# High and low activations side by side: one 512-column product with the weights' high part, halves folded on the way out of PSUM, pools at 512-byte multiples

## The chip, the cores and the metric

One NeuronCore of a Trainium2 chip runs the whole program. TensorE (PE in the profile) multiplies a stationary 128x128 operand with a moving operand of up to 512 columns and writes PSUM; its weight loads have a row of their own (PEld). VectorE (DVE), ScalarE (ACT) and GpSimd (POOL) do the rest, and SyncE (SP) issues the transfers. The metric is device time in microseconds of one execution: 2353.95 us as the median of three runs of the kernel before (2352.78 to 2354.49).

## The reference, cut to what matters

A sequence of 256 tokens of width 1024 goes through ten stages. What the change touches are products `x @ w` with the 256-token activation `x`:

```python
def swiglu(h, w_gate, w_up, w_down):           # two layers, D_FF = 2816
    return (jax.nn.silu(h @ w_gate) * (h @ w_up)) @ w_down

def swiglu_2(x, w_in, w_out):                  # four times, 4096 wide
    gate, up = jnp.split(x @ w_in, 2, axis=-1)
    return (jax.nn.silu(gate) * up) @ w_out
```

Between them stand three mixers: `even` (gated spatial mixing and latent attention), `odd` (retention) and, twice, `hyb` (gated delta rule, block attention and windowed attention, merged by gates `x @ w_gate`). Each begins with products `x @ w_in` and ends with a product into the residual. All numbers are float32, and the kernel keeps nearly that accuracy: every product is made of three, `hi*hi + hi*lo + lo*hi`, where `hi` is the operand rounded to TensorE's fp32r format and `lo` the rest.

## The kernel before

Weights stream in units of at most 128x2048 numbers. `prep` (L135) loads a unit in two halves of 128x1024 (`raw`), ScalarE casts each to `hi` (L147), VectorE subtracts to get `lo` (L148). `pump` (L153) keeps four units ahead; `hi` and `lo` have four buffers each.

The activation, transposed, is `xT`: two tiles `xh` and `xl` of [128, 8, 256], made by `new_xT` (L427) and filled by `to_T` (L403). It takes part in products in two ways:

- `block` (L284): the activation is stationary and the weights are moving, 264 to 512 columns at a time. Result: tokens by features.
- `pair_tiles` (L339) called by `apair` (L330), and the same loop written out in `chunk` of `ffn` (L595-598): the weights are stationary, and 256 columns of `xh` or `xl` move past them. Result: features by tokens. Two feature tiles share one PSUM bank of 512 columns. Per feature tile there are 8 steps of `mm3` (L230), each three products of 256 columns: `hi` with `xh`, `hi` with `xl`, `lo` with `xh`.

A feed-forward stage (`ffn`) runs over chunks of 256 features: the first two by `head` with the first form, the others by `chunk` with the second: gate and up each into one `work` bank, SiLU by ScalarE and the product by VectorE straight out of PSUM, then a split into `hp` and, one chunk later, 24 products of 512 columns into the four accumulators `y` (`emit_down`). In `ffn` and `odd` the second form writes banks of the pool `work` (four of them), in `even` and `hyb` (where `gacc` is true) banks of the pool `acc` (four as well). Each call of `apair` hands its bank to a callback `cb`: in `hyb` a causal convolution (`cb_conv`, L1095), biases, or the tanh of a gate (`cb_g`, L1152).

Which instruction stands where on an engine is decided when the program is built, by a scheduler that merges the streams; each engine then works strictly through its own list.

SBUF pools are laid out one behind the other; the constants end with `colt` (L1523), whose width follows the number of column constants. In the built program `hi`, `lo`, `raw` and the `s` tiles used as operands start 480 bytes past a multiple of 512, `xh` and `xl` 288 bytes past one.

Of the kernel before, what the change touches and what calls it, by code (L numbers as in the profile page):

```python
# [4 lines left out]
F32 = mybir.dt.float32  # L5
F32R = mybir.dt.float32r
# [10 lines left out]
TAIL = 3  # L17
ACC = 4


# [95 lines left out]
class Net:  # L116
# [15 lines left out]

    # weight stream

# [66 lines left out]

    # tiles

    def tile(self, *free, dt=F32):
        n = int(np.prod(free))
        for tag, size, bufs in (("c", 16, 24), ("c2", 64, 10), ("s1", 272, 4), ("s2", 512, 22), ("s2x", 520, 2), ("s4", 1024, 11)):
            if n <= size:
                break
        else:
            raise ValueError(n)  # L210
        t = self.sp.tile([128, size], dt, tag=tag, bufs=bufs, name=tag)
        t = t[:, 0:n]
        if len(free) == 2:
            t = t.rearrange("p (a b) -> p a b", a=free[0])
        elif len(free) == 3:
            t = t.rearrange("p (a b c) -> p a b c", a=free[0], b=free[1])
        return t
# [6 lines left out]

    # short forms

# [47 lines left out]
    def bc(self, a, m):  # L274
        """[128, n] -> [128, n, m] with a stride of zero"""
        return a.unsqueeze(2).to_broadcast([128, a.shape[1], m]) if not self.recording else a

    def bh(self, a, h):
        """[128, n] -> [128, h, n] with a stride of zero"""
        return a.unsqueeze(1).to_broadcast([128, h, a.shape[1]]) if not self.recording else a  # L280

    # products with streamed weights

# [14 lines left out]
    def group(self, n, units, xT, cb):  # L298
        """out[token, n columns] of x @ w, one block of tokens after the other"""
        self.need_x(1)  # L300
        for b in range(2):
            yield from self.block(b, n, units, xT, cb)
        self.pump()

    def opening(self, groups):
        """the first groups of a stage: the second block of tokens comes late"""
        groups = [(n, self.col_units(key, cols), cb) for n, key, cols, cb in groups]
        self.need_x(0)
        for b in range(2):
            for n, units, cb in groups:  # L310
                for i, _ in enumerate(self.block(b, n, units, self.xT, cb)):
                    if b == 0 and i == 0 and units is groups[-1][1]:
                        self.need_x(1)
                    yield

    def col_units(self, key, cols, K=8, per=4):
        """cols: column ranges, or a function of the inputs that gives the [K * 128, n] slab"""
        units = []
        n = sum(c1 - c0 for c0, c1 in cols)
        for k in range(0, K, per):  # L320
            def fn(inp, k=k):
                return kslab2(key(inp), k, k + per, *cols)
            units.append(self.unit((per, n), fn) + (per,))
        return units
# [5 lines left out]
    def apair(self, key, cols, cb):  # L330
        """out[feature, token] of x @ w for two tiles of features"""
        def fn(inp):
            return kslab2(key(inp), 0, 8, *cols)
        u = self.unit((8, 256), fn)
        self.need_x(1)
        yield from self.pair_tiles(u, 0, self.xT, 8, cb)
        self.pump()

    def pair_tiles(self, u, c0, xT, K, cb):  # L339
# [10 lines left out]
    def outproj(self, key, r0, xT, y, first, last, K=4, per=2):  # L350
        """y[block][half] += x @ w for K tiles of the rows of w from r0"""
        units = []
        for k in range(0, K, per):
            def fn(inp, k=k):
                return kslab(key(inp), r0 + k, r0 + k + per, 0, 1024)
            units.append(self.unit((per, 1024), fn))
        for b in range(2):
            for k in range(K):
                hi, lo = units[k // per]
                for n in range(2):  # L360
                    self.mm3(y[b][n], tuple(t[:, k, 128 * b:128 * b + 128] for t in xT),
                             (hi[:, k % per, 512 * n:512 * n + 512], lo[:, k % per, 512 * n:512 * n + 512]),
                             first and k == 0, last and k == K - 1)
                if k % 2 == 1 and k < K - 1:
                    yield ("part", b)
            if b == 1:
                self.pump()
            yield ("block", b)

    def outlast(self, key, r0, xTs, y, first):  # L370
        """y += x @ w for the last rows of w, four tiles per item of xTs; in the last units the first block of tokens comes first"""
        n = 2 * len(xTs)
# [12 lines left out]
        for i in range(n - TAIL):  # L385
            w = unit(i)
# [16 lines left out]
    def to_T(self, src, b, dst, n, k0=0):  # L403
        """src [128 tokens, n * 128] into dst hi/lo [128, k, 256]"""
        for q in range(0, n, 4):
            m = min(4, n - q)
            ps = self.work()
            for k in range(m):
                self.tr(ps[:, 128 * k:128 * k + 128], src[:, 128 * (q + k):128 * (q + k) + 128])
            p = ps[:, 0:128 * m].rearrange("p (k t) -> p k t", k=m)  # L410
            s = slice(k0 + q, k0 + q + m), slice(128 * b, 128 * b + 128)
            self.split(dst[0][:, s[0], s[1]], dst[1][:, s[0], s[1]], p)
# [3 lines left out]

    # ends of stages

# [8 lines left out]
    def new_xT(self):  # L427
        self.xT = tuple(self.xp.tile([128, 8, 256], F32R, tag=t, bufs=1, name=t) for t in ("xh", "xl"))

# [74 lines left out]
    def finish_out(self, b, y):  # L504
        """the last layer norm: squares about the mean of the first half, the second half comes last"""
        c = self.how[3]
        z, h, junk = self.tile(1024), self.tile(1024), self.tile(1024)
# [37 lines left out]

    # the two-matrix gated feed-forward

    def ffn(self, nt, gate, up, down, nxt):
        """gate, up: (fn of inputs -> matrix, first column); down: fn -> matrix"""
        C = nt // 2  # L550
        self.gacc = False
        y = self.new_y()
# [34 lines left out]
        def chunk(c):  # L587
            ps = []
            for src in (gate, up):
                def fn(inp, src=src):  # L590
                    w, a, z = cols(src, c)(inp)
                    return kslab(w, 0, 8, a, z)
                hi, lo = self.unit((8, 256), fn)
                p = self.work()
                for j in range(2):  # L595
                    for k in range(8):
                        self.mm3(p[:, 256 * j:256 * j + 256], (hi[:, k, 128 * j:128 * j + 128], lo[:, k, 128 * j:128 * j + 128]),
                                 (self.xT[0][:, k], self.xT[1][:, k]), k == 0, k == 7)
                ps.append(p)
                while late:  # L600
                    late.pop(0)()
                if src is gate:
                    sg = self.tile(512)
                    self.act(sg, p, AF.Silu)
                    self.pump()
# [44 lines left out]

    # softmax over the last axis of [128, H, K]

    def softmax(self, s, H, K, scale, sink=None):
        """scale: a number, or one per row and head (positive)"""
        nm = self.tile(H)
# [21 lines left out]
    def p_T(self, p, H, nk):  # L677
        """p [128 q, H, nk * 128] -> [128 k, H, nk, 128 q]"""
        pT = self.tile(H, nk, 128)
# [11 lines left out]

    # layer 0 of the first block

    def even(self, nxt):
# [81 lines left out]
        def rope(x, b, H, dst):  # L776
            """x [128, H, 32]"""
            r = rt1 if b else rt
# [169 lines left out]

    # layer 1 of the first block

# [90 lines left out]

    # the mixer of the second block

    def hyb(self, l, nxt):
# [213 lines left out]
        def task_a():  # L1258
            while "kvc" not in events:
                yield "wait"  # L1260
            M = self.masks
            # beta and g
            beta, g = self.tile(2, 4), self.tile(2, 4)
# [27 lines left out]
            yield  # L1291
            # k in token layout, normalised; v in token layout; the lengths of q
            kt, vt, rq = [None] * 2, [None] * 2, [None] * 2
# [30 lines left out]
            yield  # L1324
            # decays: from j to i in [i, j], below the diagonal times beta and with the diagonal
            Dx, DT = [None] * 2, [None] * 2
# [37 lines left out]
            yield  # L1364
            # inverse of I + A: blocks of four in closed form, then doubled; X = inverse, Y = its transpose
            X, Y, Q = ([self.tile(512) for _ in range(2)] for _ in range(3))
# [142 lines left out]

    # the whole  # L1510

    def consts(self):
# [9 lines left out]
        if not self.recording:  # L1522
            self.colt = self.cp_.tile([128, max(self.collay.n, 1)], F32, name="colt")  # L1523

# [123 lines left out]
```

## Time and profile before

| what | value |
|---|---|
| median of three runs | 2353.95 us |
| profiled execution, first to last instruction (span) | 2348.7 us |
| PE busy | 2323.6 us (99%), 15966 products |
| weight loads (PEld) | 2140.5 us (91%) |
| DVE / ACT / POOL busy | 1393.4 / 1087.6 / 92.5 us |
| granted TensorE clock | 0.998 on average, the level of 2.4 GHz |
| weights read | 416.53 MB, 53.7% of the 16 DMA engines' time |

The profiled execution spans 2348.7 us; the page gives no time for what lies around the span, so its own total is known only through the runs, whose median is 5.25 us longer. Busy time of PE counts overlapping records once: one product's record is longer than the step from its start to the next one's, so steps have to be read from the starts.

### The profile page before, as it was taken

The numbers are of one execution on the slowest core, as the hardware profiler recorded it, in microseconds if no ns is written. First come the engines' busy times: TensorE is split into PE (matmuls) and PEld (weight loads), VectorE is DVE, ScalarE is ACT, GpSimd is POOL, SyncE is SP. The second block draws the span as 40 slices with busy tenths as digits, with TensorE's granted clock in tenths as the row PEclk, the third lists the DMA queues.
The fourth block names the chain that finished last, engine by engine and source line by source line (L and its number), as shares of the span: only waits on it lengthen the run. The fifth ranks groups of instructions, "written<-read, shape, count | busy, mean of one in ns | idle before, by whom it ended". The sixth has DMA issues, their size and how long they took to land.

```text
span 2348.7 us, 38487 instructions
## 1 busy us (share of the span) xinstructions
PE 2323.6 (99%) x15966; PEld 2140.5 (91%) x15966; DVE 1393.4 (59%) x1764; ACT 1087.6 (46%) x1530; POOL 92.5 (4%) x149
## 2 busy tenths in 40 slices
PE   8999999999999999999999999999999999999998
PEld 7789988889989999999998999899999999989997
DVE  6654475565455454786666454655457875664544
ACT  6644344354444444564445444444445544453433
POOL 4200000000000000000000000000000000000000
PEclk9999999999999999999999999999999999999999
DMA  7465555555556555553365555555555533665552
GB/s 244 139 206 189 189 193 173 191 170 190 192 171 217 195 184 176 185 174 118 105 201 199 194 183 193 182 201 189 188 181 185 186 105 107 189 206 188 189 189 90
DMA packets 120575, 419.51 MB, mean 179 GB/s; under 512 B 14408, under 2 KB 17224, under 8 KB 120400
## 3 DMA queue, kind: packets, MB, share of 16 engines
q1 hardware_dynamic: 120112, 416.53, 53.7%
q8 instruction: 125, 2.05, 0.3%
q10 hardware_dynamic: 288, 0.52, 0.1%
q14 instruction: 50, 0.41, 0.1%
HBM read 415.95 MB, written 1.05 MB: 178 GB/s over the span
## 4 chain that ended last, share of the span: by engine, by line
PE 97%; DVE 1%; POOL 1%; ACT 0%; DMA 0%; issue 0%; SPq 0%; POOLq 0%; DVEq 0%; ACTq 0%
PE work L228 52%; PE acc L228 42%; PE work L236 2%; DVE lo L148 0%; DMA raw<-in_w 0%; POOL c L271 0%; ACT hi L147 0%; DVE s L251 0%; POOL c L828 0%; POOL c L827 0%; POOL c L272 0%; DVE s L239 0%; PE work L1412 0%; ACT s L258 0%; DVE xl L239 0%
## 5 line engine op out<-in xcount | busy, mean ns | idle before, releaser
L148 DVE TENSOR_TENSOR lo<-raw,hi 128x1024 fp32r<-128x1024 f32 (+3 forms) x772 | 918.3, 1209 | 564.0 <-ACT hi L147 562.3
L147 ACT CAST hi<-raw 128x1024 fp32r<-128x1024 f32 (+3 forms) x772 | 783.4, 1037 | 922.2 <-issue 667.3
L228 PE MATMUL work<-xh,hi 128*128 128x256 f32 x2496 | 699.2, 280 | 0.0
L228 PE MATMUL work<-xl,hi 128*128 128x256 f32 x2496 | 696.5, 279 | 0.0
L228 PE MATMUL work<-xh,lo 128*128 128x256 f32 x2496 | 696.4, 279 | 0.0
L228 PE MATMUL acc<-hi,s 128*128 128x512 f32 (+1 forms) x1736 | 553.4, 391 | 0.0
L228 PEld LDWEIGHTS work<-xh,hi 128*128 128x128 f32 x2496 | 468.5, 188 | 2.7
L228 PEld LDWEIGHTS work<-xl,hi 128*128 128x128 f32 x2496 | 467.1, 187 | 2.7
L228 PEld LDWEIGHTS work<-xh,lo 128*128 128x128 f32 x2496 | 469.1, 188 | 0.0
L228 PEld LDWEIGHTS acc<-hi,s 128*128 128x128 f32 x1736 | 325.7, 188 | 65.8 <-ACT s L261 0.3
L228 PE MATMUL acc<-lo,s 128*128 128x512 f32 (+1 forms) x868 | 337.6, 389 | 0.0
L228 PE MATMUL acc<-xh,hi 128*128 128x256 f32 x800 | 227.5, 284 | 0.0
L228 PE MATMUL acc<-xl,hi 128*128 128x256 f32 x800 | 223.9, 280 | 0.0
L228 PE MATMUL acc<-xh,lo 128*128 128x256 f32 x800 | 223.7, 280 | 0.0
L228 PEld LDWEIGHTS acc<-lo,s 128*128 128x128 f32 x868 | 163.1, 188 | 30.6
L239 DVE TENSOR_TENSOR s<-s,work 128x512 f32<-128x512 f32 (+1 forms) x128 | 81.0, 636 | 172.3 <-PE work L228 160.9
L228 PEld LDWEIGHTS acc<-xh,hi 128*128 128x128 f32 x800 | 150.2, 188 | 0.8 <-issue 0.5
L228 PEld LDWEIGHTS acc<-xl,hi 128*128 128x128 f32 x800 | 150.1, 188 | 0.7 <-issue 0.5
L228 PEld LDWEIGHTS acc<-xh,lo 128*128 128x128 f32 x800 | 150.2, 188 | 0.2
L228 PE MATMUL work<-hi,xh 128*128 128x512 f32 x320 | 128.6, 402 | 0.2 <-ACT xh L261 0.2
L228 PE MATMUL work<-hi,xl 128*128 128x512 f32 x320 | 126.6, 396 | 0.5 <-DVE xl L239 0.5
L228 PE MATMUL work<-lo,xh 128*128 128x512 f32 x320 | 126.5, 395 | 0.0
(117 smaller groups left out, 1949.8 us busy)
## 6 DMA issues: line engine op xcount, KB each, us to landing
raw<-in_w SPq DMA_DIRECT2D x748, 512.0 KB, 4.3
s<-in_rows SPq DMA_DIRECT2D x16, 512.0 KB, 7.4
raw<-in_w SPq DMA_DIRECT2D x12, 288.0 KB, 3.4
s<-in_rows SPq DMA_DIRECT2D x9, 256.0 KB, 5.0
raw<-in_w SPq DMA_DIRECT2D x4, 384.0 KB, 6.8
raw<-in_w SPq DMA_DIRECT2D x4, 256.0 KB, 4.4
s<-in_relb SPq DMA_DIRECT2D x2, 512.0 KB, 4.3
raw<-in_w SPq DMA_DIRECT2D x4, 240.0 KB, 2.5
```

What stands on the lines that cost most here:

```text
L147: self.nc.scalar.copy(hi[:, a:b], raw)
L148: self.nc.vector.tensor_tensor(out=lo[:, a:b], in0=raw, in1=hi[:, a:b].bitcast(F32), op=ALU.subtract)
L228: self.nc.tensor.matmul(out, lhsT=l, rhs=r, start=start, stop=stop)
L236: self.nc.tensor.transpose(out, src, self.ident)
L239: self.nc.vector.tensor_tensor(out=out, in0=a, in1=b, op=op)
```

## The change

`xh` and `xl` become the halves of one tile `x2` of [128, 8, 512]. A product in the second form is now made by `x_tile`: per step one product of 512 columns (`hi` stationary, `xh` and `xl` moving together), and one of 256 columns (`lo` stationary, `xh` moving) added to the upper half. Each feature tile therefore fills a bank of its own, and `fold` adds the two halves while they leave PSUM: a ScalarE copy of the upper half and a VectorE addition of the lower. The callbacks then read the folded tile in SBUF. Padding of `colt` and of the `s2x` tiles moves the pools, so that the operand tiles start at multiples of 512 bytes.

```diff
+LINE = 512
+FIRST = 16512
...
-        for tag, size, bufs in (("c", 16, 24), ("c2", 64, 10), ("s1", 272, 4), ("s2", 512, 22), ("s2x", 520, 2), ("s4", 1024, 11)):
+        for tag, size, bufs in (("c", 16, 24), ("c2", 64, 10), ("s1", 272, 4), ("s2", 512, 22), ("s2x", 544, 2), ("s4", 1024, 11)):
...
     def apair(self, key, cols, cb):
...
-        yield from self.pair_tiles(u, 0, self.xT, 8, cb)
+        ps = []
+        for j in range(2):
+            ps.append(self.x_tile(u, j))
+            if j == 0:
+                yield
+        t = self.tile(512)
+        for j in range(2):
+            self.fold(t, j, ps[j])
+        cb(t)
+        yield
         self.pump()
+
+    def x_tile(self, u, j):
+        ps = self.acc() if self.gacc else self.work()
+        c = slice(128 * j, 128 * j + 128)
+        for k in range(8):
+            self.mm(ps, u[0][:, k, c], self.x2[:, k], k == 0, False)
+            self.mm(ps[:, 256:512], u[1][:, k, c], self.xT[0][:, k], False, k == 7)
+        return ps
+
+    def fold(self, t, j, ps):
+        o = t[:, 256 * j:256 * j + 256]
+        self.cp(o, ps[:, 256:512])
+        self.add(o, ps[:, 0:256], o)
...
     def new_xT(self):
-        self.xT = tuple(self.xp.tile([128, 8, 256], F32R, tag=t, bufs=1, name=t) for t in ("xh", "xl"))
+        self.x2 = self.xp.tile([128, 8, 512], F32R, tag="x2", bufs=1, name="x2")
+        self.xT = self.x2[:, :, 0:256], self.x2[:, :, 256:512]
...
-                hi, lo = self.unit((8, 256), fn)
-                p = self.work()
+                u = self.unit((8, 256), fn)
+                p = self.tile(512)
                 for j in range(2):
-                    for k in range(8):
-                        self.mm3(p[:, 256 * j:256 * j + 256], (hi[:, k, 128 * j:128 * j + 128], lo[:, k, 128 * j:128 * j + 128]),
-                                 (self.xT[0][:, k], self.xT[1][:, k]), k == 0, k == 7)
+                    self.fold(p, j, self.x_tile(u, j))
...
-            self.colt = self.cp_.tile([128, max(self.collay.n, 1)], F32, name="colt")
+            fixed = 512 + 3584 + 64 + FIRST
+            self.colt = self.cp_.tile([128, max(self.collay.n, 1) + -(fixed + 4 * self.collay.n) % LINE // 4], F32, name="colt")[:, 0:max(self.collay.n, 1)]
```

The order of TensorE's products at the start of a chunk of the first feed-forward stage shows the new pattern; a row names out, then moving and stationary operand, each with its buffer's number. Before:

```order
L228 MATMUL acc_1272<-hi_1637,s2_1600 128x512
L228 MATMUL work_1841<-xh_1181,hi_1671 128x256
L228 MATMUL work_1841<-xl_1182,hi_1671 128x256
L228 MATMUL work_1841<-xh_1181,lo_1672 128x256
L228 MATMUL work_1841<-xh_1181,hi_1671 128x256
L228 MATMUL work_1841<-xl_1182,hi_1671 128x256
L228 MATMUL work_1841<-xh_1181,lo_1672 128x256
```

And in the changed kernel at the same place:

```order
L230 MATMUL acc_1250<-hi_1595,s2_1558 128x512
L230 MATMUL work_1780<-x2_1160,hi_1629 128x512
L230 MATMUL work_1780<-x2_1160,lo_1630 128x256
L230 MATMUL work_1780<-x2_1160,hi_1629 128x512
L230 MATMUL work_1780<-x2_1160,lo_1630 128x256
```

Two steps of `k` take six products before and four now; `hi` is loaded once in a step instead of twice.

On VectorE, the start of the convolutions of the first `hyb` stage stood like this before (`s2x` is the padded input of a convolution, `lo` rows are weight splits):

```order
L254 TENSOR_SCALAR s2_9274<-s2x_9272,colt_81 128x256
L251 SCALAR_TENSOR_TENSOR s2_9274<-s2x_9272,colt_81,s2_9274 128x256
L254 TENSOR_SCALAR s2_9274<-s2x_9272,colt_81 128x256
L251 SCALAR_TENSOR_TENSOR s2_9274<-s2x_9272,colt_81,s2_9274 128x256 x4
L148 TENSOR_TENSOR lo_9287<-raw_9288,hi_9286 128x1024
L251 SCALAR_TENSOR_TENSOR s2_9274<-s2x_9272,colt_81,s2_9274 128x256
L148 TENSOR_TENSOR lo_9287<-raw_9292,hi_9286 128x1024
```

and now:

```order
L150 TENSOR_TENSOR lo_8531<-raw_8532,hi_8530 128x1024
L241 TENSOR_TENSOR s2_8510<-acc_8493,s2_8510 128x256
L256 TENSOR_SCALAR s2_8518<-s2x_8516,colt_80 128x256
L150 TENSOR_TENSOR lo_8531<-raw_8536,hi_8530 128x1024
L253 SCALAR_TENSOR_TENSOR s2_8518<-s2x_8516,colt_80,s2_8518 128x256 x2
L256 TENSOR_SCALAR s2_8518<-s2x_8516,colt_80 128x256
L253 SCALAR_TENSOR_TENSOR s2_8518<-s2x_8516,colt_80,s2_8518 128x256 x2
L241 TENSOR_TENSOR s2_8574<-acc_8540,s2_8574 128x256
L253 SCALAR_TENSOR_TENSOR s2_8518<-s2x_8516,colt_80,s2_8518 128x256
```

The folds (`s2<-acc,s2`) stand among the convolution's steps and the weight splits, and a fold of the next pair (`s2_8574`) comes before the last steps of this one.

## Rows read from the trace of the kernel before

**Rows 1.** The page: busy time, granted clock by slice, engines of the chain that ended last.

```profile
PE 2323.6 (99%) x15966; PEld 2140.5 (91%) x15966; DVE 1393.4 (59%) x1764; ACT 1087.6 (46%) x1530; POOL 92.5 (4%) x149
...
PEclk9999999999999999999999999999999999999999
...
PE 97%; DVE 1%; POOL 1%; ACT 0%; DMA 0%; issue 0%; SPq 0%; POOLq 0%; DVEq 0%; ACTq 0%
```

**Rows 2.** Groups by line and shape: out<-moving,stationary, count | busy us, mean ns | idle.

```profile
L228 PE MATMUL work<-xh,hi 128*128 128x256 f32 x2496 | 699.2, 280 | 0.0
...
L228 PE MATMUL acc<-hi,s 128*128 128x512 f32 x1712 | 546.4, 392 | 0.0
...
L228 PE MATMUL acc<-lo,s 128*128 128x512 f32 x856 | 333.5, 390 | 0.0
L228 PE MATMUL acc<-xh,hi 128*128 128x256 f32 x800 | 227.5, 284 | 0.0
...
L228 PE MATMUL work<-hi,xh 128*128 128x512 f32 x320 | 128.6, 402 | 0.2 <-ACT xh L261 0.2
...
L228 PE MATMUL acc<-s,hi 128*128 128x256 f32 x384 | 70.5, 285 | 0.0
L228 PE MATMUL acc<-s,lo 128*128 128x256 f32 x192 | 54.5, 284 | 0.0
L228 PE MATMUL acc<-hi,xh 128*128 128x512 f32 x80 | 32.5, 406 | 0.0
```

**Rows 3.** Timeline of PE, a chunk and its down products: start us, us, instruction.

```profile
159.73 0.28 PE L228 MATMUL work<-xh,hi 128*128 128x256 f32 x1
...
171.04 0.40 PE L228 MATMUL acc<-hi,s 128*128 128x512 f32 x1
...
176.51 0.28 PE L228 MATMUL work<-xh,hi 128*128 128x256 f32 x1
```

**Rows 4.** The same view where the activation is stationary.

```profile
396.50 0.40 PE L228 MATMUL work<-hi,xh 128*128 128x512 f32 x1
...
407.70 0.62 PE L228 MATMUL work<-s,s 128*128 128x512 f32 x2
```

**Rows 5.** The same view, 256 moving columns of another tile in `hyb`.

```profile
1172.39 0.48 PE L228 MATMUL acc<-s,hi 128*128 128x256 f32 x2
...
1183.98 0.28 PE L228 MATMUL acc<-xh,hi 128*128 128x256 f32 x1
```

**Rows 6.** The same view, 264 moving columns, four steps of k.

```profile
966.59 0.28 PE L228 MATMUL acc<-hi,xh 128*128 128x264 f32 x1
...
966.96 0.28 PE L228 MATMUL acc<-hi,xh 128*128 128x264 f32 x1
...
967.32 0.28 PE L228 MATMUL acc<-hi,xh 128*128 128x264 f32 x1
...
967.67 0.28 PE L228 MATMUL acc<-hi,xh 128*128 128x264 f32 x1
...
968.04 0.39 PE L228 MATMUL acc<-hi,xh 128*128 128x512 f32 x1
```

**Rows 7.** Groups by shape: reads of 256 columns of PSUM by ACT and DVE.

```profile
L239 DVE TENSOR_TENSOR s<-s,work 128x256 f32<-128x256 f32 x24 | 10.0, 417 | 11.4 <-ACT s L258 11.4
...
L261 ACT COPY s<-acc 128x256 f32<-128x256 f32 x4 | 1.5, 372 | 5.4 <-DVE s L239 5.4
```

**Rows 8.** Windows: busy us and count by engine, clock, DMA share, GB/s.

```profile
725.00:925.00 200.00, 200.00 (x1428) 188.25 (x1427) 100.10 (x94) 83.59 (x95) 0.00 (x0) 1.00 0.57 188
984.00:1020.00 36.00, 36.00 (x308) 36.00 (x307) 35.63 (x78) 22.72 (x34) 0.97 (x6) 1.00 0.56 183
```

**Rows 9.** What PE waited for, whole span: us, times, longest.

```profile
PE work L236 <- DVE s L251: 10.0, 4, 8.7
```

**Rows 10.** Timeline of PE, a stretch of 256-column products in another rhythm.

```profile
143.72 0.28 PE L228 MATMUL work<-xh,hi 128*128 128x256 f32 x1
...
148.82 0.39 PE L228 MATMUL acc<-hi,s 128*128 128x512 f32 x1
```

## The prediction, made before the changed kernel ran

> **What bounds the kernel now.** I read the page first [rows 1]. PE is busy 99% of the span, the clock stands at its upper level in every slice, and the chain that ended last is PE for 97%. No other engine passes 59%, and the largest entry in the list of what PE waited for is 10.0 us [rows 9]. So time is the number of products times the step between them; whatever is done elsewhere counts only where it makes PE wait.
>
> Then the groups by shape [rows 2]. The second form has 2496 + 800 = 3296 steps of k, each with three products of 256 columns, 9888 of PE's 15966. Their mean duration of 280 ns says little, as records overlap; the timeline has the steps [rows 3]. From 159.73 to 171.04 stand the 96 products of a chunk: 11.31 / 96 = 117.8 ns each, 353.4 ns for a step of k. From 171.04 to 176.51 stand 24 products of 512 columns: 5.47 / 24 = 227.9 ns. With the activation stationary [rows 4], 48 products of 512 columns take 11.20 / 48 = 233.3 ns. And 96 products that move 256 columns of another tile [rows 5] take 11.59 / 96 = 120.7 ns.
>
> From 117.8 and 227.9 comes the estimate that carries the rest: 256 columns cost 110.1 ns, and a product costs 7.7 ns that do not depend on its columns. The change keeps the columns (768 per step of k) and drops one product of three. That is a gain of a few ns per step, not of a third.
>
> **The change part by part.**
>
> *The products.* A step of k becomes one product of 512 columns and one of 256. The nearest rows are 227.9 [rows 3], where moving and stationary tiles start at the same offset from a multiple of 512 bytes, as all will now, and 117.8: together 345.7, so 7.7 ns less. Times 3296 this is 25.4 us. The bounds are wide, since the trace has no 512 columns of the activation beside these weights: 220.2 + 110.1 = 330.3 if the fixed part goes altogether (76 us less), 233.3 + 120.7 = 354.0 by the dearest rows (2 us more).
>
> The Trainium skill, "TensorE: Matmul & The Clock Gate", section "Back-to-back issue gap", puts the warm gap at N / 2.4 + 2.5 ns, so 215.8 and 109.2 ns here. The trace disagrees, with 227.9 and 117.8. By that rule only 2.5 ns go with a product: 8 us in all, a third of my term.
>
> *The places of the tiles.* Where the activation is stationary, its tile (288 bytes past a multiple of 512) and the weights (480) start at different offsets, and a product takes 233.3 ns; where both are at 480 it takes 227.9. After the change all are at 0. I take the 5.4 ns for the 3 x (320 + 80) = 1200 products of 512 columns of that form [rows 2]: 6.5 us. Bounds: nothing, if offsets don't matter; and if starting on a multiple is worth the whole fixed part, 13.1 x 1200 + 7.7 x 2568 (the products with stationary `s`, 1712 + 856) = 35 us, and some 6 us more for the 384 + 192 = 576 of the form in [rows 5], counted in [rows 2]. On the other side, if 512 columns with `s` go to 233.3, 14 us lost.
>
> One row speaks against any worth of the multiple as such: in the 264-column products the moving row starts at 480, 0, 32 and 64 bytes past a multiple, step of k by step of k, and three products take 0.37, 0.36, 0.35 and 0.37 us [rows 6]. The one that starts on the multiple is no faster. But its stationary operand was still off.
>
> The Trainium skill, "SBUF — State Buffer", in its box on SBUF cachelines, knows lines of 16 bytes. All the old starts are multiples of 32. By that rule the moved pools change nothing, and the 6.5 us fall away.
>
> *The folds.* There are 3296 / 8 = 412 feature tiles, each with one ScalarE copy and one VectorE addition of 256 columns out of PSUM, at 372 and 417 ns [rows 7]: 153 us for ACT and 172 us for DVE in all, on engines with 1087.6 and 1393.4 us. In the feed-forward stages, which hold 148 of the 206 pairs (two per chunk of the second form: 9 chunks in two stages, 14 in four), 200 us have 100.1 us of DVE and 83.6 of ACT [rows 8]. A chunk takes 11.31 + 5.47 = 16.8 us, so 12 chunks with 4 folds each add 20 and 18 us: both stay near 60%. A chunk now fills four `work` banks instead of two, all there are, but a bank is wanted again only after three other tiles (2.8 us each) and the down products (5.5 us). PE's work hides the folds; without that cover a fold would show 0.8 us.
>
> The exception is `hyb`. During its six convolution pairs DVE is busy 35.63 of 36 us [rows 8]. Each pair adds 0.83 us to an engine that is full, while PE gets 0.1 us faster. Twelve pairs in two layers make 10 us. What queues behind a fold is the convolution and the weight splits, and PE waits for the bank: a pair takes two of four `acc` banks, so the third pair needs the first pair's folded. It has one pair's time in hand (5.5 us), less the folds' own 1.2 us and whatever split of 1.2 us stands ahead. Some of the 10 us is absorbed there. In the gate pairs and elsewhere, where tasks' products wait for DVE [rows 9], I expect a little. I take 8 us, bounds 0 and 25 (the 24 convolution and bias pairs of both layers fully exposed, 20 us, and 5 for the tasks).
>
> *The rest.* The weight stream, its casts and splits are the same instructions; the callbacks read SBUF instead of PSUM, which I put at nothing. DMA share is 0.57 in the feed-forward window and grows by about 1%.
>
> *Sum.* -25.4 - 6.5 + 8 = -24 us. The profiled span of 2348.7 us would become 2324.8; with the 5.25 us between the span and the median, 2330 us.
>
> **The rivals.**
>
> *The multiple of 512 is worth the fixed part of every product.* For it: the fixed cost does depend on the pair of tiles (227.9 against 233.3, 117.8 against 120.7), so it looks like operands being read; in one stretch products like those of [rows 3] run in another rhythm, 45 products in 5.10 us, 113.3 ns each [rows 10], so 117.8 is no floor; and no row has both operands on a multiple. Against it: [rows 6]. Then 23.1 x 3296 = 76 us, 35 and 6 us, less 8 for the folds: 109 us less, 2245 us. Chance 0.18; a part of it may come as well, so times between 2245 and 2315 belong here.
>
> *The pairing gets dearer.* 512 columns of `x2` stream while the weights are loaded from a tile that starts at the same offset. If the two reads hinder each other, a product of 512 columns takes 233.3 or more and one of 256 takes 120.7: the step of k costs 354.0, the first term turns to +2, the 6.5 us are lost, and the folds remain: 2364 us. It decides from about 350.7 ns per step of k on, where the products' gain no longer pays 8 us of folds. For it: a pairing that costs 5.4 ns more exists in this trace. Against: those tiles start at different offsets. Chance 0.15.
>
> *VectorE becomes the bound in `hyb`.* With the full 25 us of stalls and the products as forecast: 2354 - 32 + 25 = 2347. For it: 35.63 of 36 us. Against: PE's waits for DVE are small now, and four banks stand between. Chance 0.12.
>
> *The change does not do what it says.* If what a product costs beyond its columns belongs to the columns after all (the 7.7 ns is a difference of two means), the 25.4 us vanish and only the 6.5 us against 8 us of folds are left: 2355. Chance 0.08.
>
> **How the numbers follow.** The forecast has 0.47; its own range, with the stalls from 0 to 16 us and the products between half the term and one and a half of it, is 2310 to 2350. For 8 in 10 the range reaches down to 2240, since the first rival is the largest single move, and up to 2358, which leaves out most of the second rival. A change of over 0.2%, 4.7 us, can be told from none, so faster means below 2349.2 and slower above 2358.7. Faster: the forecast nearly whole (0.45), the first rival (0.18), two thirds of the third (0.08), and a little of the fourth (0.03): 0.74. Same: the remainders of the forecast, the third and the fourth: 0.10. Slower: the second rival (0.14) and the tail of the third (0.02): 0.16.
>
> **What would show it right or wrong.** In the timeline of a chunk, 64 products in 32 x 345.7 ns = 11.06 us where 96 took 11.31; a chunk near 10.6 us means the first rival, one of 11.3 the second. In the products with stationary activation, 228 instead of 233 ns. In the list of PE's waits, entries of `acc` for DVE in the two `hyb` stages of some us. DVE near 1565 us and ACT near 1240. I am wrong if PE's waits grow by more than 25 us, or if the step of k lies outside 330 to 354 ns.

## The result and the profile after

The changed kernel takes 2366.95 us (2366.35 to 2368.7, four runs). The ratio to the kernel before is 1.0058, 95% interval 1.0044 to 1.0072: slower by 13 us, where I forecast 24 us faster. The profiled execution has a span of 2364.6 us.

The page of the changed kernel, the lines that answer [rows 1]:

```profile
PE 2328.1 (98%) x12670; PEld 1991.7 (84%) x12670; DVE 1523.5 (64%) x2176; ACT 1232.0 (52%) x1942; POOL 94.2 (4%) x149
...
PEclk9999999999999999999999999999999999999999
...
PE 96%; DVE 1%; POOL 1%; issue 0%; DMA 0%; ACT 0%; SPq 0%; POOLq 0%; DVEq 0%; ACTq 0%
```

PE has 3296 products fewer and bounds the kernel as it did, yet its busy time did not fall. The timeline of PE says why. A chunk in the changed kernel, to be held against [rows 3] (start us, us, instruction):

```profile
162.20 0.39 PE L230 MATMUL work<-x,hi 128*128 128x512 f32 x1
...
172.43 0.40 PE L230 MATMUL work<-x,hi 128*128 128x512 f32 x1
172.67 0.28 PE L230 MATMUL work<-x,lo 128*128 128x256 f32 x1
172.79 0.40 PE L230 MATMUL work<-x,hi 128*128 128x512 f32 x1
...
173.49 0.40 PE L230 MATMUL acc<-hi,s 128*128 128x512 f32 x1
```

From 162.20 to 173.49 stand 32 steps of k: 11.29 / 32 = 352.8 ns, where three products took 353.4. Read by starts, a wide product takes 0.24 us and a narrow one 0.12 (236.0 and 116.8 ns, means over all 2496 pairs that write `work`). A product is gone from every step, and only 0.6 ns with it.

The products with stationary activation, to be held against [rows 4], in the same view:

```profile
362.71 0.39 PE L230 MATMUL work<-hi,x 128*128 128x512 f32 x1
...
373.60 0.27 PE L238 MATMUL work<-ident,s 128*128 128x128 f32 x1
```

48 products in 10.89 us are 226.9 ns; they took 233.3. This term came as forecast. What PE waited for (us, times, longest), beside [rows 9]:

```profile
PE work L238 <- DVE s L253: 10.9, 3, 9.9
PE work L230 <- ACT s L263: 9.9, 3, 3.5
PE work L238 <- DVE s L241: 3.8, 2, 2.1
```

The two lower lines are new, and one of the kernel before has shrunk to 0.7 us, a wait at 76 us:

```profile
PE work L228 <- DVE s L251: 4.0, 1, 4.0
```

There PE now waits 2.8 us for ACT, the third wait of the second line. The other two and the third line lie in the two `hyb` stages, 10.9 us, and over the whole lists PE's waits grew from 16.8 to 27.9 us. Windows of the changed kernel, a feed-forward stretch and the convolutions of the first `hyb` as in [rows 8], and one window in each `hyb`; under them the two `hyb` windows of the kernel before (window, us, busy us and count of PE, PEld, DVE, ACT, POOL, granted clock, DMA share, GB/s):

```profile
725.00:925.00 200.00, 200.00 (x1050) 170.41 (x1049) 115.14 (x142) 100.13 (x142) 0.00 (x0) 1.00 0.56 188
984.00:1020.00 36.00, 36.00 (x205) 31.20 (x205) 35.96 (x75) 27.27 (x49) 0.64 (x6) 1.00 0.56 182
...
975.00:1045.00 70.00, 64.83 (x372) 55.26 (x370) 62.45 (x133) 47.48 (x84) 4.87 (x10) 0.98 0.61 203
1845.00:1910.00 65.00, 59.75 (x326) 49.10 (x325) 52.65 (x112) 33.35 (x72) 5.15 (x6) 0.92 0.43 138
```

```profile
975.00:1045.00 70.00, 70.00 (x591) 68.94 (x590) 60.05 (x125) 42.69 (x69) 4.29 (x10) 1.00 0.60 202
1845.00:1910.00 65.00, 65.00 (x474) 58.36 (x473) 50.43 (x88) 34.30 (x72) 4.08 (x6) 1.00 0.41 135
```

In the feed-forward stretch PE has no gap, and none in the convolutions, though DVE is busy 35.96 of their 36 us. Over the two `hyb` windows it had none before; now it loses 5 us in each, behind the convolutions, and the granted clock falls. The timeline of the first gap in the changed kernel:

```profile
1037.21 0.63 PE L238 MATMUL work<-ident,s 128*128 128x128 f32 x4
...
1037.59 0.48 PE L230 MATMUL acc<-x,hi 128*128 128x512 f32 x1
...
1037.91 0.28 PE L230 MATMUL acc<-x,lo 128*128 128x256 f32 x1
1038.15 1.04 ACT L149 CAST hi<-raw 128x1024 fp32r<-128x1024 f32 x1 [0.81 <-ACT hi L149]
...
1039.59 1.03 ACT L149 CAST hi<-raw 128x1024 fp32r<-128x1024 f32 x1
1039.98 0.69 DVE L241 TENSOR_TENSOR s<-work,c 128x512 f32<-128x512 f32 x1 [1.19 <-POOL c L274]
1040.52 0.65 ACT L263 COPY s<-acc 128x256 f32<-128x256 f32 x2
...
1041.05 0.61 ACT L263 COPY s<-work 128x512 f32<-128x512 f32 x1
...
1041.71 0.65 PE L230 MATMUL work<-s,s 128*64 128x256 f32 x4 [3.53 <-ACT s L263]
```

PE stands for 3.5 us until ACT has copied `work` out. In ACT's list two weight casts, an activation and the two copies of a fold (`s<-acc`, x2) stand ahead of that copy; the fold's copies take 0.53 us of the gap (1040.52 to 1041.05). The same place in the kernel before:

```profile
1034.38 0.60 PE L236 MATMUL work<-ident,s 128*128 128x128 f32 x4
...
1035.78 0.61 ACT L261 COPY s<-work 128x512 f32<-128x512 f32 x1
...
1039.27 0.65 PE L228 MATMUL work<-s,s 128*64 128x256 f32 x4
```

There the copy ended 1.4 us after the transposes (`ident`), and it ends 3.8 us after them now. But there PE's list also had 37 products of the second form between the transposes and the products that need the copy, 4.5 us of work, and it has 2 now. The second `hyb` has the same 37 and 2. So the gap is a longer wait with less work to cover it. And after the gap, in a window of the changed kernel:

```profile
1042.30:1052.54 10.24, 8.10 (x33) 6.88 (x32) 6.83 (x18) 3.97 (x14) 2.11 (x2) 0.50 0.43 130
```

For 10.24 us the granted clock is 0.50, the 1.2 GHz level: it fell 0.6 us after the gap of 3.5 us had ended, and a second wait, of 2.1 us, lies within. In the second `hyb` it fell at 1878.5 us, 0.6 us before a gap of 3.5 us ended, for 10.24 us again. The page's slices of 59 us don't show it.

Summed over PE's records, each from its start to the next start (us, before and after):

| products | before | after | difference |
|---|---|---|---|
| second form into `work` (2496 steps of k) | 881.8 | 880.6 | -1.1 |
| second form into `acc` (800 steps) | 288.8 | 296.0 | +7.1 |
| stationary activation, 512 columns (1200) | 284.8 | 278.6 | -6.2 |
| down products with `s` (2567 records) | 590.9 | 594.0 | +3.1 |
| small f32 products and transposes, `hyb`'s waits among them | 178.3 | 189.4 | +11.1 |
| start of the first product, and the rest | | | +2.0 |

That makes 16 us, as the spans do (2364.6 - 2348.7).

### The profile page after: what moved, and what is told of

The parts are those of the page before. It is cut to its first block, busy times and chain, and to the rows that moved or that the text cites. A ratio compares the mean times of both kernels' runs of the same rounds, so it can differ in the third digit from the quotient of the medians.

```text
span 2364.6 us, 32735 instructions
## 1 busy us (share of the span) xinstructions
PE 2328.1 (98%) x12670; PEld 1991.7 (84%) x12670; DVE 1523.5 (64%) x2176; ACT 1232.0 (52%) x1942; POOL 94.2 (4%) x149
## 4 chain that ended last, share of the span: by engine, by line
PE 96%; DVE 1%; POOL 1%; issue 0%; DMA 0%; ACT 0%; SPq 0%; POOLq 0%; DVEq 0%; ACTq 0%
PE work L230 51%; PE acc L230 42%; PE work L238 3%; DVE lo L150 1%; POOL c L273 0%; DMA raw<-in_w 0%; POOL c L274 0%; DVE s L241 0%; POOL c L853 0%; POOL c L852 0%; DVE s L253 0%; ACT s L260 0%; DVE c L1323 0%; ACT hi L149 0%; PE work L1437 0%
## 5 line engine op out<-in xcount | busy, mean ns | idle before, releaser
L230 PE MATMUL work<-x,hi 128*128 128x512 f32 x2496 | 884.1, 398 | 0.0
L230 PE MATMUL work<-x,lo 128*128 128x256 f32 x2496 | 700.5, 281 | 0.0
L230 PEld LDWEIGHTS work<-x,hi 128*128 128x128 f32 x2496 | 468.9, 188 | 115.0
L230 PEld LDWEIGHTS work<-x,lo 128*128 128x128 f32 x2496 | 471.3, 189 | 2.7
L230 PE MATMUL acc<-x,hi 128*128 128x512 f32 x800 | 288.6, 403 | 0.0
L230 PE MATMUL acc<-x,lo 128*128 128x256 f32 x800 | 224.9, 281 | 0.0
L230 PE MATMUL work<-hi,x 128*128 128x512 f32 x640 | 205.4, 394 | 0.6 <-DVE x L241 0.5
L241 DVE TENSOR_TENSOR s<-s,s 128x512 f32<-128x512 f32 (+3 forms) x234 | 152.2, 658 | 64.9 <-ACT s L263 54.5
L241 DVE TENSOR_TENSOR s<-work,s 128x256 f32<-128x256 f32 (+5 forms) x382 | 165.0, 435 | 27.3 <-ACT s L263 14.3
L230 PEld LDWEIGHTS acc<-x,lo 128*128 128x128 f32 x800 | 152.0, 190 | 0.2
L230 PEld LDWEIGHTS work<-hi,x 128*128 128x128 f32 x640 | 119.9, 188 | 26.6 <-DVE x L241 1.8
```

The costliest lines, as they stand in the source:

```text
L230: self.nc.tensor.matmul(out, lhsT=l, rhs=r, start=start, stop=stop)
L241: self.nc.vector.tensor_tensor(out=out, in0=a, in1=b, op=op)
```

## The experiments

Theories: **places** (the time of a product depends on where its two operands start), **turn** (a wide and a narrow product in turn are dearer than each in a series), **folds** (the new reads of PSUM hold PE up in `hyb`). The start of a tile is told in bytes past a multiple of 512; the distance is the start of the weights less that of x, 192 in the kernel before. Every run was timed beside the kernel before, 2353.3 to 2353.8 us.

**1. The places alone.** The kernel before with the moved tiles and nothing else:

```
+LINE = 512
+FIRST = 16512
...
-("s2x", 520, 2)
+("s2x", 544, 2)
...
-self.colt = self.cp_.tile([128, max(self.collay.n, 1)], ...)
+fixed = 512 + 3584 + 64 + FIRST
+self.colt = self.cp_.tile([128, max(self.collay.n, 1) + -(fixed + 4 * self.collay.n) % LINE // 4], ...)
```

> The kernel before with the padding of the change alone: products as before, tiles at multiples of 512 bytes. Theory A (the 5.5 ns that products with the activation stationary lost in the changed kernel, 233 to 227.5, come from the places alone): 1200 x 5.5 = 6.6 us less, about 2347 us, with 227 to 228 ns for these products and 117.8 for the 256-column ones. Rival (they come from the two halves lying in one tile x2): no change, 233 ns.

Measured 2367.95 us, ratio 1.0062 (1.005 to 1.0075). A chunk in the timeline of this kernel:

```profile
161.19 0.28 PE L230 MATMUL work<-xh,hi 128*128 128x256 f32 x1
...
172.70 0.40 PE L230 MATMUL acc<-hi,s 128*128 128x512 f32 x1
```

11.51 / 96 = 119.9 ns where it was 117.8. All 9888 products lost 2.2 ns, 22 us (sums +16.9 and +4.9), and the stationary activation gained its 6.3. I had seen only the second half: moving tiles to equal starts is a loss in sum.

**2. The change without the places.** The changed kernel with tiles where they were:

```
-("s2x", 544, 2)
+("s2x", 520, 2)
...
-fixed = 512 + 3584 + 64 + FIRST
-self.colt = self.cp_.tile([128, max(self.collay.n, 1) + -(fixed + 4 * self.collay.n) % LINE // 4], ...)
+self.colt = self.cp_.tile([128, max(self.collay.n, 1)], ...)
```

> The changed kernel without the padding: tiles at 480 and x2 at 288 bytes past a multiple of 512. Theory A: 6 to 7 us slower than the changed kernel, about 2373 us, stationary-activation products back at 233 ns, the step of k (512 + 256 columns) as in the changed kernel, near 352 to 353 ns. Rival (the two streams hinder each other because x2 and the weights start at the same offset, and that is why the 512-column product beside hi takes 235.5 ns): the 512-column product falls to 228 or rises beyond 236, and the step of k moves by 5 ns or more (16 us).

Measured 2361.53 us, 1.0035 (1.0023 to 1.0048). A chunk:

```profile
161.59 0.40 PE L230 MATMUL work<-x,hi 128*128 128x512 f32 x1
...
172.76 0.39 PE L230 MATMUL acc<-hi,s 128*128 128x512 f32 x1
```

11.17 / 32 = 349.1 ns. I had expected 352 to 353 ns and 2373 us: the places count for the new step too. Better than equal starts, and still slower than before.

**3. Wide, then narrow.** The changed kernel, eight and eight:

```
             self.mm(ps, u[0][:, k, c], self.x2[:, k], k == 0, False)
+        for k in range(8):
             self.mm(ps[:, 256:512], u[1][:, k, c], self.xT[0][:, k], False, k == 7)
```

> The changed kernel with the order in x_tile changed alone: eight products of 512 columns, then eight of 256. Theory B (the gain was lost because narrow and wide products alternate: the load of the next weights has only a narrow product to hide behind, and the wide one waits for it): wide products 227 to 229 ns, narrow 117.8, a step of k 345 to 346, 3296 x 7 = 23 us less than the changed kernel, about 2344 us. Rival (moving x2 beside hi is dear by itself): wide products stay at 235 ns, time within 5 us of 2367.

Measured 2348.92 us, 0.9982 (0.9974 to 0.9991): 18 us less than the changed kernel, by the order of the same instructions. A chunk:

```profile
161.17 0.39 PE L230 MATMUL work<-x,hi 128*128 128x512 f32 x1
...
172.32 0.40 PE L230 MATMUL acc<-hi,s 128*128 128x512 f32 x1
```

11.15 / 32 = 348.4 ns, where 345 to 346 and 2344 us were expected. The gaps in `hyb` and the stretches at clock 0.50 are still there (from 1034.4 and 1863.9), so the turn is a cost apart from the folds.

**4. The old form in the `acc` stages.** The changed kernel, with this in front of the new form:

```
+        if self.gacc:
+            yield from self.pair_tiles(u, 0, self.xT, 8, cb)
+            self.pump()
+            return
```

> The changed kernel, but in the stages whose results go to the pool acc (even and both hyb) the second form is made as before (three products of 256 columns per step, callbacks straight from PSUM); feed-forward and odd stages as changed. Theory C (the folds in hyb sit in VectorE's full list and cost PE some 15 to 18 us): 15 to 18 us less than the changed kernel, about 2350 us, PE's stalls near 1030 and 1880 us back from 9 us each to 2. Rival (the loss is spread over all folds): at most 5 us less.

Measured 2351.66 us, 0.9993 (0.9984 to 1.0002), 15.3 us less than the changed kernel. The two windows of this kernel:

```profile
975.00:1045.00 70.00, 70.00 (x571) 67.98 (x570) 59.82 (x128) 42.80 (x78) 4.31 (x10) 1.00 0.58 194
1845.00:1910.00 65.00, 65.00 (x469) 58.22 (x468) 49.60 (x89) 34.65 (x72) 4.08 (x6) 1.00 0.42 134
```

PE is full again and the clock stays up; over its whole list it waits 16.5 us, against 27.9 in the changed kernel. The new form costs 15 us there, gaps and slow clock together. The three products per step of k are back as well; as these take longer here (360 ns against 353, 5 us for 800 steps), they cannot be what gained, and without them the rest of the new form would cost some 21 us, an estimate. That rest is the folds, the second bank of each pair and the order of PE's list (the 37 products of cover are back), which this run doesn't part.

**5. Both edits, equal starts.** Runs 3 and 4 in one.

> The changed kernel with two edits at once: eight products of 512 columns and then eight of 256 per tile of features, instead of the two in turn, and the old form of three products with its one addition in the stages that accumulate in `acc`. If the turn of wide and narrow (some 4 to 5 ns per step of k) and the folds in `hyb` (15 us) are two causes that add up, the 2351.7 us of the run with the old form alone fall by 2368 steps x 4 to 5 ns: 2340 to 2342 us, and the stretches of granted clock 0.5 are gone. If the order only pays where it eases the folds, nothing adds to the old form's 15 us: 2349 to 2352 us.

Measured 2338.67 us, 0.9938 (0.9926 to 0.9951). The two causes add up; no stretch at clock 0.50 is left but one of 3.41 us at 78 us, which the kernel before has too, and the end. (The trace has 2496 steps into `work` and 800 into `acc`; the 2368 and 928 of this and a later expectation were counted by stage, and the difference is under 1 us.)

**6 and 7. Where x stands, in the kernel before.** One number each, x at 480 and at 224:

```
-("s2x", 520, 2)
+("s2x", 544, 2)      (6: x at 480, distance 0 from the weights)
+("s2x", 576, 2)      (7: x at 224, distance 256)
```

> The kernel before with the tiles of x moved to 480 bytes past a multiple of 512, where the weights and activations stand already; nothing else. If what a product costs hangs on the start of the moving operand relative to the stationary one, this repeats the run with all tiles on multiples: 120.0 ns for the 9888 products of 256 columns (117.7 before), 227 ns with stationary activation (233.3 before), 9888 x 2.3 ns less 1200 x 5.8 ns = 16 us more, about 2369 us. If the multiple of 512 itself matters, neither rate changes where no tile stands on one: 2353 us.

> The kernel before with the tiles of x at 224 bytes past a multiple of 512, 256 bytes away from the 480 of the other tiles. If only an equal start is slow for 256 columns and only a distance of 192 is slow for 512, this place has both low rates, 117.7 and 227 ns: 1200 x 5.8 ns = 7 us less, about 2346 us. If any unequal start is alike, the time stays at 2353 us with 117.7 and 233.3 ns. If the cost grows with the distance, both rates leave the known values, and the trace says which way.

Measured 2367.29 us, 1.0061 (1.0048 to 1.0073), and 2368.67 us, 1.0065 (1.0052 to 1.0079). A chunk of run 6 and one of run 7:

```profile
160.34 0.28 PE L228 MATMUL work<-xh,hi 128*128 128x256 f32 x1
...
171.86 0.40 PE L228 MATMUL acc<-hi,s 128*128 128x512 f32 x1
```

```profile
159.69 0.28 PE L228 MATMUL work<-xh,hi 128*128 128x256 f32 x1
...
171.20 0.40 PE L228 MATMUL acc<-hi,s 128*128 128x512 f32 x1
```

Both repeat run 1: 11.52 / 96 = 120.0 and 11.51 / 96 = 119.9 ns for 256 columns, 226.8 for the stationary activation (48 products, 362.64 to 373.53 in run 6). No tile stands on a multiple of 512 here, so it is the distance between the two starts that counts, not the multiple; and 256 is as 0. My hope for run 7, the low rate in both forms, fell.

**8. Both edits at the old places.** Run 5 without the padding, as in run 2.

> The run with both edits (wide before narrow, old form in the `acc` stages), with the tiles at their old places: x2 at 288 and the others at 480 bytes past a multiple of 512. The theory of the relative start: the old triples in `acc` return from 120.0 to 117.7 ns (928 steps x 7 ns = 6 us less), the stationary activation from 227 to 233.3 ns (7 us more), and the rest hangs on what 512 columns of x2 cost beside unequal weights: at 227.9 ns beside narrow ones of 117.7 it is about 2333 us, at 233.3 ns about 2346 us. If the places don't matter once wide and narrow don't take turns, it equals the aligned run of both within 2 us.

Measured 2336.14 us, 0.9927 (0.9914 to 0.9939), nearest to the first case, which gave 2333. A chunk:

```profile
161.60 0.40 PE L230 MATMUL work<-x,hi 128*128 128x512 f32 x1
...
172.69 0.39 PE L230 MATMUL acc<-hi,s 128*128 128x512 f32 x1
```

11.09 / 32 = 346.6 ns, with wide products at 229.9 and narrow ones at 116.6 (means). The sum is the 345.7 of the prediction within 1 ns; its parts, 227.9 and 117.8, are 2.0 under and 1.2 over.

**9 and 10. Two more distances.** Run 8 with x2 at 352 (distance 128) and at 416 (distance 64):

```
-("s2x", 520, 2)
+("s2x", 528, 2)      (9: x2 at 352)
+("s2x", 536, 2)      (10: x2 at 416)
```

> The run with both edits at the old places (2336 us), with x2 at 352 instead of 288 bytes past a multiple of 512: 128 away from the 480 of the other tiles, where it was 192. Distances 0 and 256 gave the same rates, 192 others. If the cost repeats every 128 bytes, this is distance 0 again: 120.0 ns for the triples in `acc`, 227 ns with stationary x2, and the time of the aligned run of both, 2339 us. If it repeats every 256, 128 is a new value; if any distance that is not a multiple of 256 is alike, 117.7 and 233 ns, 2336 us.

> The same with x2 at 416, 64 bytes from the 480 of the other tiles. If 64 and 192 are alike (a repeat every 128), 117.7 ns for the triples in `acc` and 233 ns with stationary x2, 2336 us. If the repeat is 256, the two rates may be others; a place with 117.7 and 227 ns would give 2336 less 1200 x 6 ns = 2329 us. If the distance matters only where it is 192, it is 120.0 and 227 ns, 2339 us.

Measured 2348.02 us, 0.9976 (0.9966 to 0.9986), and 2325.13 us, 0.988 (0.9865 to 0.9895). Run 10 is the fastest of all, 29 us below the kernel before and 42 below the changed one. Its chunk and its stationary activation:

```profile
159.96 0.39 PE L230 MATMUL work<-x,hi 128*128 128x512 f32 x1
...
171.06 0.39 PE L230 MATMUL acc<-hi,s 128*128 128x512 f32 x1
```

```profile
358.35 0.39 PE L230 MATMUL work<-hi,x 128*128 128x512 f32 x1
...
369.34 0.27 PE L238 MATMUL work<-ident,s 128*128 128x128 f32 x1
```

11.10 / 32 = 346.9 ns and 10.99 / 48 = 229.0 ns. Neither is the lowest of its kind. What gains over run 8 is the old triples in `acc`, 281.2 us in all where run 8 has 288.8, and the stationary activation, 280.2 for 284.8; the wide and narrow pairs lose 1.9. Neither expectation named 128 as the dear place; each distance has its own rates, and a repeat every 128 bytes is excluded. All of these, in ns (256 columns: the narrow products into `work`, means; in run 7 the triples):

| distance of the starts | run | 512 of x2, moving | 256, moving | 512, x stationary |
|---|---|---|---|---|
| 0 | 5 | 229.7 | 119.1 | 226.8 |
| 64 | 10 | 233.1 | 114.2 | 229.0 |
| 128 | 9 | 232.8 | 118.5 | 232.4 |
| 192 | 8 | 229.9 | 116.6 | 233.4 |
| 256 | 7 | - | 120.0 | 226.8 |

In the last column x is the stationary operand, so the sign of the distance is the other one there. Told as moving less stationary, and with 256 taken as 0, the rows 64 and 192 change places in the two middle columns, and both forms of 512 columns then rise alike over 0, 64, 128 and 192: 229.7, 229.9, 232.8, 233.1 and 226.8, 229.0, 232.4, 233.4. No run turns the sign of the distance round to test this reading.

**11. In twos.** The changed kernel with two wide, two narrow:

```
-        for k in range(8):
-            self.mm(ps, u[0][:, k, c], self.x2[:, k], k == 0, False)
-            self.mm(ps[:, 256:512], u[1][:, k, c], self.xT[0][:, k], False, k == 7)
+        for k in range(0, 8, 2):
+            for i in (k, k + 1):
+                self.mm(ps, u[0][:, i, c], self.x2[:, i], i == 0, False)
+            for i in (k, k + 1):
+                self.mm(ps[:, 256:512], u[1][:, i, c], self.xT[0][:, i], False, i == 7)
```

> The changed kernel with two products of 512 columns and then two of 256, instead of one and one; nothing else. If each change between wide and narrow costs, the 8 changes per tile of features stand between the 16 of the changed kernel (2367 us) and the 2 of the run with eight and eight (2349 us): 18 us x 8 / 14 = 10 us less, 2357 us. If only a narrow product alone between two wide ones is dear, nearly the whole 18 us go, 2350 us. If what the order of eights gained was that the second half of the weights was wanted later, little is gained, 2363 to 2367 us.

Measured 2349.41 us, 0.9982 (0.9973 to 0.9991). A chunk:

```profile
160.96 0.62 PE L230 MATMUL work<-x,hi 128*128 128x512 f32 x2
161.41 0.40 PE L230 MATMUL work<-x,lo 128*128 128x256 f32 x2
...
172.09 0.40 PE L230 MATMUL acc<-hi,s 128*128 128x512 f32 x1
```

11.13 / 32 = 347.8 ns, all of the gain of eights. So it is not each change of width that costs, but the strict alternation. The reason given in the expectation of run 3, a wide product that waits for weights loaded behind a narrow one, would hold for every second wide product here too; nothing of it shows, and what in the alternation costs stays open.

**12. Three products, x at 416.** The kernel before with the one number of run 10:

```
-("s2x", 520, 2)
+("s2x", 536, 2)
```

> The kernel before, three products of 256 columns per step of k everywhere, with the tiles of x at 416 bytes past a multiple of 512 (64 from the 480 of the others); no side-by-side product, no fold beyond its own, nothing else. If the place is what pays and the wide product does not, 9888 products at about 114 ns where they took 117.7 are 35 us less, 1200 with stationary activation at about 229 instead of 233.3 are 5 us less: 2314 us, below the 2325 us of the run that has wide products at this place, because 3 x 114 = 342 ns is less than the 347 ns of its wide and narrow pair. If the wide product is worth something at this place too, the old form stays above 2325 us. If the quick rhythm of the triples in `acc` there came from their short series and does not hold over 96 products, 117.7 ns stay: 2345 to 2353 us.

Measured 2336.37 us, 0.9929 (0.9916 to 0.9943): 17 us for one number, where I expected 40 and 2314 us. The timeline has two series of the same products in two rhythms:

```profile
160.09 0.28 PE L228 MATMUL work<-xh,hi 128*128 128x256 f32 x1
...
171.40 0.39 PE L228 MATMUL acc<-hi,s 128*128 128x512 f32 x1
...
323.43 0.28 PE L228 MATMUL work<-xh,hi 128*128 128x256 f32 x1
...
345.22 0.59 PE L228 MATMUL work<-s,s 128*128 128x256 f32 x2
```

11.31 / 96 = 117.8 ns behind the down products, 21.79 / 192 = 113.5 ns behind stationary activation, from weight tiles at the same addresses. At this distance both rhythms can hold, for a whole series. All 62 series into `work` that follow down products run at the slower one, and 13 of the other 15 at the quick one. I took the quick one for the place's own rate, and the feed-forward chunks don't have it. Over all, three products into `work` take 352.2 ns (mean), and the wide and narrow pair of run 10 takes 347.3: the side-by-side product is worth 5 ns per step of k there.

## Why the prediction was wrong

*The products' term failed.* It was to give 7.7 ns per step of k, 25.4 us, and a chunk's step gave 0.6 (353.4 to 352.8), 1.1 us over all steps into `work`. I added the rates of two series, 227.9 and 117.8, and called the sum a step of k. Chunks by order and by place (ns per step of k, runs 8, 2, 5 and the changed kernel; run 5's chunk is that of run 3):

| | old places | equal starts |
|---|---|---|
| wide and narrow in series | 346.6 | 348.4 |
| in turn | 349.1 | 352.8 |

In series at the old places the sum was right to 1 ns, in part by luck: the 227.9 came from equal starts, and the errors of the two parts cancel (run 8). Of the 7.1 ns that the change lacks, 6.2 come from two conditions that I carried over without a row: the turn (4.4 ns at equal starts, 2.5 at the old places) and the equal starts (1.8 ns in series, 3.7 in turn). The trace had [rows 5], 120.7 ns from two tiles that both start at 480, and I used it as a bound and in a rival only, though every product of 256 columns was about to get that relation. What [rows 3 to 5] could have told is that equal starts are good for one form and bad for another. The runs then have the loss in series in the narrow product (116.6 to 119.1 ns from distance 192 to 0), the gain in the stationary activation (233.4 to 226.8), and the wide product alike at both (229.9 and 229.7).

*The multiple of 512 is worth nothing.* Runs 1, 6 and 7 agree within 1.4 us with and without it. The first rival falls, and [rows 6] had said so.

*The stationary activation came as priced*, 5.4 ns forecast, 6.4 in the timeline, 6.2 us for 6.5. The Trainium skill, "SBUF — State Buffer", box on SBUF cachelines, has lines of 16 bytes. By that alone all these runs would be alike, as every start is a multiple of 32; moving x2 alone takes them from 2325 to 2348 us (runs 8 to 10).

The Trainium skill, "TensorE: Matmul & The Clock Gate", section "Step-by-step: what each phase is for", says that PE reads moving and stationary operands through two ports, so that loading the next weights takes no read bandwidth from the running product. If the two reads had nothing to do with each other, a step would not depend on the distance of their starts. In the runs it does, by 3% where x is stationary: 64 bytes, from distance 192 to 256, take 6.6 ns from a step (233.4 to 226.8). What in the reads does it, no run here shows.

*The folds were sized at 8 us, and the new form cost 15 net in the `acc` stages* (run 4), some 21 without what its products gain there. The stage was right, and the way was not. I had PE waiting in the convolution pairs for an `acc` bank that DVE folds late. DVE is full there, as forecast, and PE has no gap; its list of waits has no `acc` bank that waits for DVE, the entry that I named as a sign. The waits stand behind the convolutions, where products of the tasks want what ACT and DVE make of a `work` bank, and PE's list has 2 products of cover instead of 37. No part of the prediction speaks of the order of PE's list, and no run parts it from the folds.

What I also left out is what a gap does behind itself: the granted clock at 0.50 for 10.24 us, twice. PE is busy 8.10 us in the first such stretch; at the upper level the same work would take about half, so up to 4 us of each belong to the clock, an estimate. With the 11 us of waits that is most of the 21. Elsewhere the folds are hidden, as forecast: PE is busy all of 725 to 925 us. DVE came to 1523.5 us and not 1565, though the work on it grew as forecast: 312 additions out of `work` take 417 ns each and the rest out of `acc` 416, and the durations of all its records rose by 168 us. Records overlap, and busy time counts an overlap once.

*The second rival, "the pairing gets dearer", came nearest*: 354.0 ns and 2364 us, against 352.8 and 2366.95. It was right in the step by luck: it had 233.3 and 120.7 ns, and the changed kernel has 236.0 and 116.8. I had it that the stationary products would lose too, and they gained; the waits and the slow clock of the new form cost some 13 us more than the 8 and made up for it. And more than half of the dearness is the turn, of which no part of the prediction speaks. (The step from which this rival was to decide is 351.0 ns by its own terms, 353.4 less 8 us over 3296 steps, not 350.7.) The range ended at 2358 and left most of this rival out.

## What to carry to other kernels

A rate read from a series holds for that series: its neighbours, its order and the places of its operands. Before products of different widths are mixed, keep those of a kind together, two at least, and before tiles are moved to round addresses, look for a row in the trace that already has the relation that the move creates. When PE is full, a gap of some microseconds is paid twice, once as waiting and once as a lower clock.

## What was not expected of the hardware

- A step of PE depends on the distance between the starts of its moving and stationary tiles, differently for 256 and 512 columns: 114.2 to 120.0 ns and 226.8 to 233.4 ns. Distances 0 and 256 are alike; 0, 64, 128 and 192 differ in two columns of the table at least.
- At one distance, 64, the same products run at 117.8 or at 113.5 ns for a whole series; into `work`, with two exceptions, the slower one stands behind down products. [Rows 10] has the second rhythm too: 113.3 ns in the kernel before, at distance 192, behind a step of 200 ns from the start of a series. What chooses it stays open.
- Wide and narrow in strict turn cost 4.4 ns per pair over eights; in twos, nothing.
- A gap of 3.5 us brought 10.24 us at the 1.2 GHz level in both `hyb` stages of the changed kernel, once from 0.6 us after its end and once from 0.6 us before it; in run 4, where PE stayed busy there, the clock stayed up. The kernel before has 3.41 us at this level behind its gap of 4.0 us at 76 us.
